# Hybrid attention, DeltaNet and SSD step on one core: norms split around their root, pinned weight casts, three banks for turned tiles, sign and copies of the softmax stage

## The chip, the cores and the metric

One core of one Trainium2 chip runs the whole program. The metric is the device time of one execution in microseconds (us); the median of several executions counts. Matrix products run on TensorE (PE in the profile, its weight loads PEld), elementwise work on VectorE (DVE), ScalarE (ACT) and GpSimd (POOL); SyncE (SP) issues most transfers.

## The reference, cut to what matters

Two request groups, 128 context tokens and 512 latent tokens, pass through the same two layers with the same weights (model width 1024, fp32):

```python
for layer in range(DEPTH):
    h = modulate(x, norm_mix_g[layer], sh1, sc1)      # rms_norm(x) * gain * (1 + scale) + shift
    y = even_mixer(h) if layer % 2 == 0 else odd_mixer(h)
    x = x + g1 * y
    h = modulate(x, norm_mlp_g[layer], sh2, sc2)
    x = x + g2 * (relu(h @ w_mlp_in) ** 2) @ w_mlp_out
return rms_norm(x, final_norm_g)
```

The even mixer joins grouped-query attention (8 heads of 64, 2 key heads; `softmax(q k * 64 ** -0.5) v`; latent queries see 512 latent and 256 cached keys) with a bidirectional gated DeltaNet (4 heads, state 128 x 128, a chunk recurrence in each direction). The odd mixer is a bidirectional Mamba-2 SSD. Besides the two outputs the new caches and states are returned.

## The kernel before, in words

Tokens are 5 tiles of 128 (tile 0 is context). Every large product is computed in three passes from a split of each fp32 operand into a rounded high part and a remainder: high by high, high by low, low by high. For weights, `wpart` (L267) makes the high part on ACT (L272) and the remainder on DVE (L275). `gemm` (L291, products L300) makes feature-major outputs of 128 rows for half of the tokens; `by_rows` (L317, products L328) makes token-major outputs, 512 columns at a time.

**Norms between blocks.** In the last pass of a `by_rows` with `done`, the 24 products of one token tile t run, then `gated` (L357) multiplies the PSUM result by the gate (L363, or L365) and adds it to x (L366), ACT squares x and sums the row (L381), and `done(t)` (L415) runs. For t = 1, 2 and 4 it computes the reciprocal root of tiles 0 and 1, of tile 2, and of tiles 3 and 4 together: `root` (L383) is 12 DVE instructions on a column or two, each needing the one before (L384, L234, L235, three rounds of L237 to L239). `scaled` (L397) then writes, for each tile and half row, x * root * scale (L402) and adds the shift (L403). The half rows live in four buffers. `turned` (L406) transposes a half row on PE in four pieces (L409) into one PSUM bank, copies it rounded on ACT (L412) and takes the remainder on DVE (L413). At t = 2 the half rows of tiles 0 and 1 are turned, at t = 3 those of tile 2; `late` (L428) turns tiles 3 and 4 between the first products of the next block.

This happens three times: after the even layer's output projection, where the bank of `turned` comes from a pool of two (L796, L797); after the first MLP, where `late` (the inner function, L828) prepares the odd layer's norm and the same lambda draws from a pool of one bank (L822); and after the odd layer's output projection, again with two (L1339, L1340). The next block's first products read the turned columns of tiles 0, 1 and 2.

**Order.** Each engine works through one queue in order. The queues are filled at build time by a scheduler that takes, among the instructions it holds to be ready, the one traced first; `issue_after(ins)` forces an instruction behind `ins` on its engine. Two engines that access the same PSUM bank are ordered by a semaphore.

**Attention and DeltaNet.** Both run in one stage: `attention` (L1211) is a generator whose steps are traced between the first DeltaNet head and the other three. For each of 4 pairs of heads it turns q (L1238 copies the result), and for each token tile computes scores into PSUM (L1243), the row maximum (L1249), its product with -scale (L1250), the exponential with row sums (L1252), the reciprocal (L1253) and the division (L1255); the probabilities are transposed (L1294) and copied out of PSUM alternately by DVE and ACT (L1297), then multiplied by v (L1303). The scores have one buffer and the transposes one bank. The probabilities' ring lies in the two landing buffers of the weights.

`delta_head` (L917) ends with the recurrence: per chunk and direction PE forms the new values in a bank (L1094, L1095), DVE makes a scaled copy `vk` (L1098) and a plain copy `vn` (L1100), PE multiplies `vk` by the keys into the other half of the same bank (L1102), and DVE updates the state (L1104); `vn` enters the output (L1107). The context chunk does the same (L1120, L1122, L1124, with the state copied by ACT at L1126).

Of the kernel before, what the change touches and what calls it, by code (L numbers as in the profile page):

```python
# [11 lines left out]
F32 = mybir.dt.float32  # L12
F32R = mybir.dt.float32r
I32 = mybir.dt.int32
AF = mybir.ActivationFunctionType
# [187 lines left out]
class Prog:  # L203
    def __init__(self, nc, tc, ctx, io, widx, pidx, cidx, csmall, taps=None):
        self.nc, self.tc, self.ctx, self.io = nc, tc, ctx, io
        self.turn, self.share = 0, False
        self.turns = [], None
        self.behind = None
        self.mlast = None
        self.widx, self.pidx, self.cidx, self.csmall = widx, pidx, cidx, csmall  # L210
        self.taps = taps or {}
# [55 lines left out]
    def wpart(self, raw, c, m=P, pool=None):  # L267

        pool = pool or self.wp
        hi = pool.tile([P, KT, m], F32R, name="whi", tag="whi")  # L270
        lo = pool.tile([P, KT, m], F32R, name="wlo", tag="wlo")
        self.nc.scalar.copy(out=hi, in_=raw[:, :, c:c + m])  # L272
        self.turn += 1
        eng = self.nc.gpsimd if self.share and self.turn % 2 else self.nc.vector
        eng.tensor_tensor(out=lo, in0=raw[:, :, c:c + m], in1=hi.bitcast(F32), op=ALU.subtract)  # L275
        return hi, lo
# [113 lines left out]
    def modulated(self, pool, scale, shift, h, off):  # L390


        nc, v = self.nc, self.nc.vector
        square, root = self.norm_rows(pool)
        todo = []

        def scaled(t, r):  # L397
            q = min(t, 1)
            for j in range(2):
                y = self.wp.tile([P, 512], F32, name="hrow", tag="hrow", bufs=4)  # L400
                c = slice(j * 512, j * 512 + 512)
                v.scalar_tensor_tensor(out=y, in0=self.x[:, t, c], scalar=r[:, t:t + 1], in1=scale[:, q, c], op0=ALU.mult, op1=ALU.mult)  # L402
                v.tensor_tensor(out=y, in0=y, in1=shift(q, j), op=ALU.add)  # L403
                todo.append((t, 4 * j, y))

        def turned(t, a, y):  # L406
            ps = self.bank("hps")
            for k in range(4):
                nc.tensor.transpose(ps[:, k * P:(k + 1) * P], y[:, k * P:(k + 1) * P], self.ident)  # L409
            ps = ps.rearrange("p (k c) -> p k c", c=P)  # L410
            hi, lo = (x[:, a:a + 4, off[t]:off[t] + P] for x in h)
            self.mlast = nc.scalar.copy(out=hi, in_=ps)  # L412
            v.tensor_tensor(out=lo, in0=ps, in1=hi.bitcast(F32), op=ALU.subtract)  # L413

        def done(t):  # L415
            if t in (2, 3):
                while todo:
                    turned(*todo.pop(0))
            if t in (1, 2, 4):
                a = 2 if t == 2 else t - 1  # L420
                r = root(a, t + 1)
                for u in range(a, t + 1):
                    scaled(u, r)
            self.turns = todo, turned

        return square, done
# [285 lines left out]
    def even(self):  # L712
# [108 lines left out]
        with ExitStack() as e1:  # L821
# [6 lines left out]
            def late():  # L828
                for _ in side:
                    pass  # L830
                shift, scale = (self.bands(mraw.tile([P, 2048], F32, name="bands", tag="wraw").rearrange("p (q c) -> p q c", q=2), 1, kind) for kind in (0, 1))
                self.padding(np_, h)
                square, done = self.modulated(np_, scale, lambda q, j: shift[:, q, j * 512:j * 512 + 512], h, TOFF)
                sq.append(square)
                return done
# [81 lines left out]
    def delta_head(self, dn, pd, h, st_, gt):  # L917
# [171 lines left out]
        for n in range(4):  # L1089
            for d in range(2):  # L1090
# [8 lines left out]
                vn = dn.tile([P, P], F32, name="vn", tag=f"vn{d}", bufs=2)  # L1099
                v.tensor_copy(vn, pv[:, 0:P])  # L1100
                if n < 3:
# [14 lines left out]
        for d in range(2):  # L1116
# [4 lines left out]
            vn = dn.tile([P, P], F32, name="vn0", tag=f"vn{d}", bufs=2)  # L1121
            v.tensor_copy(vn, pv[:, 0:P])  # L1122
            vns.append(vn)
# [87 lines left out]
    def attention(self, at, psc, pacc, qkv, keys, ota):  # L1211
# [10 lines left out]
        def stacks(kv, pr):  # L1222
# [4 lines left out]
            for ts_ in ((0, 1), (2, 3), (4,)):  # L1227
# [7 lines left out]
                for j, t in enumerate(ts_):  # L1235
                    for i in range(2):
                        nc.tensor.transpose(pt[:, (i * n + j) * P:(i * n + j + 1) * P], hf[:, j, i], self.ident)
                nc.scalar.copy(out=qs[:, :, ts_[0] * P:(ts_[0] + n) * P], in_=pt[:, :2 * n * P].rearrange("p (i c) -> p i c", i=2))  # L1238
            return qs
# [5 lines left out]
        def softmax(sc, p):  # L1245

            n = sc.shape[1]
            mx, sm = (at.tile([P, 2], F32, name=m, tag=m, bufs=3)[:, :n] for m in ("amx", "asm"))
            v.tensor_reduce(out=mx, in_=sc, axis=AX.X, op=ALU.max)  # L1249
            v.tensor_scalar(out=mx, in0=mx, scalar1=-scale, scalar2=None, op0=ALU.mult)  # L1250
            for i in range(n):
                nc.scalar.activation(out=p[:, i], in_=sc[:, i], func=AF.Exp, scale=scale, bias=mx[:, i:i + 1], accum_out=sm[:, i:i + 1])  # L1252
            v.reciprocal(out=sm, in_=sm)  # L1253
# [7 lines left out]
        for kv in range(2):  # L1261
            for pr in range(2):
# [17 lines left out]
                for t in range(1, NT):  # L1280
# [9 lines left out]
                    for j in range(3):  # L1290
# [5 lines left out]
                        turn += 1  # L1296
                        (v.tensor_copy if turn % 2 else nc.scalar.copy)(out=dst, in_=quad(pt))  # L1297
                    yield
# [446 lines left out]
```

## Time and profile before

| what | value |
|---|---|
| median of 3 runs | 2155.83 us (2148.13 to 2157.08) |
| the profiled execution's own time | 2143.07 us |
| its span, first to last instruction | 2141.2 us |
| mean granted TensorE clock | 0.968 |
| PE busy | 2029.4 us (95%) |
| DVE busy | 1376.8 us (64%) |
| ACT busy | 935.4 us (44%) |

A busy PE is a PE with a product in its pipe, not one at its peak. The granted clock is 1.00 at 2.4 GHz and 0.50 at 1.2 GHz; values between are a stretch with both.

### The profile page before, as it was taken

The page shows a single profiled execution, that of the slowest core. Times are in us where ns is not written, and L with a number is a line of the kernel's source. Part 1 is how long each engine was busy: PE and PEld are TensorE (multiplying, and loading weights), DVE is VectorE, ACT ScalarE, POOL GpSimd, SP SyncE. Part 2 cuts the span into 40 slices and gives each one's busy share as a digit, 9 for nine tenths or more (in the row PEclk, how much of TensorE's full clock was granted, in tenths as well). Part 3 has the DMA queues.
Part 4 walks back from the last instruction along what each step waited for, and adds up shares of the span by engine and source line. Part 5 has one row for each costly group of instructions (what it writes and reads, how often), then busy time and mean ns, then how long its engine had stood idle before and what let it go on. Part 6 is the DMA issues. An engine that isn't in the chain of part 4 may idle for free.

```text
span 2141.2 us, 32845 instructions
## 1 busy us (share of the span) xinstructions
PE 2029.4 (95%) x13227; PEld 1827.7 (85%) x13227; DVE 1376.8 (64%) x2628; ACT 935.4 (44%) x1959; POOL 147.3 (7%) x106
## 2 busy tenths in 40 slices
PE   6999698898899999999899999999999899999998
PEld 4989686775797989898799999999888888989896
DVE  6386777874886767664678886787634634343445
ACT  4344457573342423233259866666531332323131
POOL 1031302100000000000000001111110000000000
PEclk9999789898999999999999999999999999999999
DMA  7261101005255343332234343333341221212121
GB/s 328 85 241 40 38 1 35 1 12 198 100 188 190 134 148 136 141 124 95 89 101 148 129 146 120 114 133 126 117 159 67 91 97 60 79 60 99 59 79 50
DMA packets 55834, 233.31 MB, mean 109 GB/s; under 512 B 6074, under 2 KB 21186, under 8 KB 33922
## 3 DMA queue, kind: packets, MB, share of 16 engines
q1 hardware_dynamic: 45952, 216.63, 28.4%
q10 hardware_dynamic: 9730, 14.58, 1.9%
q8 instruction: 104, 1.70, 0.3%
q14 instruction: 48, 0.39, 0.1%
HBM read 222.76 MB, written 8.43 MB: 108 GB/s over the span
## 4 chain that ended last, share of the span: by engine, by line
PE 85%; DVE 9%; DMA 2%; ACT 2%; issue 1%; POOL 0%; ACTq 0%; SPq 0%; DVEq 0%; POOLq 0%
PE gps L300 41%; PE rps L328 28%; PE yps L1648 2%; PE atps L750 2%; PE offps L1662 1%; PE scps L1243 1%; PE dps L1032 1%; DMA X<-growd 1%; PE stps L1679 1%; DMA wraw<-wall 1%; PE avps L1303 1%; PE dps L1038 1%; PE ptps L1294 1%; DVE wlo L275 1%; PE xkps L1498 1%
## 5 line engine op out<-in xcount | busy, mean ns | idle before, releaser
L300 PE MATMUL gps<-hh,whi 128*128 128x322 f32 (+3 forms) x1552 | 488.6, 316 | 1.4 <-ACT hh L412 1.4
L300 PE MATMUL gps<-hh,wlo 128*128 128x322 f32 (+3 forms) x1552 | 486.5, 314 | 0.0
L300 PE MATMUL gps<-hl,whi 128*128 128x322 f32 (+3 forms) x1552 | 485.6, 313 | 0.0
L300 PEld LDWEIGHTS gps<-hh,whi 128*128 128x128 f32 (+1 forms) x1552 | 292.3, 189 | 7.9 <-issue 5.1
L300 PEld LDWEIGHTS gps<-hl,whi 128*128 128x128 f32 (+1 forms) x1552 | 292.4, 188 | 3.2 <-issue 2.8
L300 PEld LDWEIGHTS gps<-hh,wlo 128*128 128x128 f32 (+1 forms) x1552 | 292.4, 188 | 2.1 <-issue 1.7
L328 PE MATMUL rps<-wlo,hidh 128*128 128x512 f32 x640 | 253.3, 396 | 0.0
L328 PE MATMUL rps<-whi,hidh 128*128 128x512 f32 x640 | 252.3, 396 | 0.0
L328 PE MATMUL rps<-whi,hidl 128*128 128x512 f32 x640 | 250.5, 395 | 0.0
L272 ACT CAST whi<-wraw 128x1024 fp32r<-128x1024 f32 (+2 forms) x132 | 140.3, 1065 | 247.1 <-PE rps L328 176.3
L284 DVE TENSOR_TENSOR wlo<-wraw,whi 128x1024 fp32r<-128x1024 f32 x88 | 107.4, 1225 | 191.5 <-ACT whi L283 191.5
L300 PE MATMUL gps<-yh,whi 128*128 128x320 f32 x1024 | 227.1, 311 | 0.2 <-ACT yh L412 0.2
L275 DVE TENSOR_TENSOR wlo<-wraw,whi 128x1024 fp32r<-128x1024 f32 (+3 forms) x123 | 157.8, 1283 | 100.7 <-ACT whi L272 100.3
L283 ACT CAST whi<-wraw 128x1024 fp32r<-128x1024 f32 x88 | 91.8, 1049 | 269.6 <-PE rps L328 188.5
L300 PEld LDWEIGHTS gps<-yh,whi 128*128 128x128 f32 x1024 | 172.6, 189 | 1.0 <-ACT yh L412 0.7
L300 PE MATMUL gps<-yh,wlo 128*128 128x320 f32 x512 | 158.6, 310 | 0.0
L328 PEld LDWEIGHTS rps<-whi,hidh 128*128 128x128 f32 x640 | 120.3, 188 | 29.3 <-issue 1.2
L328 PEld LDWEIGHTS rps<-wlo,hidh 128*128 128x128 f32 x640 | 120.3, 188 | 28.8 <-issue 0.6
L328 PEld LDWEIGHTS rps<-whi,hidl 128*128 128x128 f32 x640 | 120.3, 188 | 28.6
L485 DVE SCALAR_TENSOR_TENSOR macc<-wraw,condst,macc 128x512 f32<-128x512 f32 x196 | 137.2, 752 | 5.6 <-ACT macc L488 5.6
L650 DVE TENSOR_SCALAR hr<-gps 128x320 f32<-128x320 f32 x128 | 62.9, 492 | 105.7 <-PE gps L300 105.6
L651 ACT ACTIVATE hr<-hr 128x320 f32<-128x320 f32 x128 | 60.2, 470 | 150.8 <-DVE hr L650 149.3
(412 smaller groups left out, 3509.7 us busy)
## 6 DMA issues: line engine op xcount, KB each, us to landing
wraw<-wall SPq DMA_DIRECT2D x158, 1024.0 KB
bc<-afs SPq DMA_DIRECT2D x40, 512.0 KB
Q<-afr SPq DMA_DIRECT2D x64, 128.0 KB
xt<-xt ACTq DMA_DIRECT2D x1, 2560.0 KB
X<-growd SPq DMA_DIRECT2D x8, 320.0 KB
x<-x ACTq DMA_DIRECT2D x1, 2560.0 KB
xd<-x ACTq DMA_DIRECT2D x1, 2560.0 KB
x<-xd SPq DMA_DIRECT2D x1, 2560.0 KB
```

The costliest lines, as they stand in the source:

```text
L272: self.nc.scalar.copy(out=hi, in_=raw[:, :, c:c + m])
L275: eng.tensor_tensor(out=lo, in0=raw[:, :, c:c + m], in1=hi.bitcast(F32), op=ALU.subtract)
L283: self.nc.scalar.copy(out=hi, in_=x)
L284: self.nc.vector.tensor_tensor(out=lo, in0=x, in1=hi.bitcast(F32), op=ALU.subtract)
L300: self.nc.tensor.matmul(ps, ws[k // KT][q // 2][:, k % KT, :], xs[q % 2][k][:, c], start=k == 0 and q == 0, stop=k == n - 1 and q == 2)
L328: nc.tensor.matmul(ps, parts[x][k][:, c], w[y][:, j, :], start=k == 0 and q == 0, stop=k == n - 1 and q == 2)
L485: nc.vector.scalar_tensor_tensor(out=a, in0=x, scalar=w, in1=a, op0=ALU.mult, op1=ALU.add)
L650: nc.vector.tensor_scalar(out=r, in0=ps, scalar1=0.0, scalar2=None, op0=ALU.max)
L651: nc.scalar.activation(out=r, in_=r, func=AF.Square)
L750: nc.tensor.matmul(ps[:, :n], x[k][:, TOFF[t]:TOFF[t] + P], w[:, k, :], start=k == 0 and q == 0, stop=k == KT - 1 and q == 2)
L1032: nc.tensor.matmul(py[:, t * 32:(t + 1) * 32], m32[:, t, :], mixed(Xc, t, l), start=True, stop=True)
L1648: nc.tensor.matmul(py[q * 64:q * 64 + 64, pr * P:(pr + 1) * P], X[t](1 + d)[:, hh * 64:hh * 64 + 64], D[t][:, d, hh, :], start=d == 0, sto ...
```

## The change

In `scaled`, x * scale is computed first, for all half rows of the call, before `root` is; then one instruction multiplies by the root and adds the shift. At t = 4 four of these last instructions are kept, and the next four calls of `wpart` have their DVE remainder forced behind them: two behind tile 2's second half row, two behind tile 3's. For the norm after the first MLP, `turned` takes banks in turn from three pools (one bank, one bank, and the products' pool of six). In the softmax stage q is multiplied by -scale when it is copied out of PSUM, so that the scores are negative: the row minimum is then the bias itself and the product at L1250 is gone. `vn` is copied by ACT, and three of four copies of the transposed probabilities are ACT's.

```diff
@@ wpart
-        eng.tensor_tensor(out=lo, in0=raw[:, :, c:c + m], in1=hi.bitcast(F32), op=ALU.subtract)
+        with self.tc.issue_after(self.hold.pop(0).ins) if self.hold else nullcontext():
+            eng.tensor_tensor(out=lo, in0=raw[:, :, c:c + m], in1=hi.bitcast(F32), op=ALU.subtract)
@@ modulated
-        todo = []
-        def scaled(t, r):
-            q = min(t, 1)
-            for j in range(2):
-                y = self.wp.tile([P, 512], F32, name="hrow", tag="hrow", bufs=4)
-                c = slice(j * 512, j * 512 + 512)
-                v.scalar_tensor_tensor(out=y, in0=self.x[:, t, c], scalar=r[:, t:t + 1], in1=scale[:, q, c], op0=ALU.mult, op1=ALU.mult)
-                v.tensor_tensor(out=y, in0=y, in1=shift(q, j), op=ALU.add)
+        todo, held = [], []
+        def scaled(a, b):
+            ys = []
+            for t in range(a, b):
+                for j in range(2):
+                    y = self.wp.tile([P, 512], F32, name="hrow", tag="hrow", bufs=4)
+                    c = slice(j * 512, j * 512 + 512)
+                    v.tensor_tensor(out=y, in0=self.x[:, t, c], in1=scale[:, min(t, 1), c], op=ALU.mult)
+                    ys.append((t, j, y))
+            r = root(a, b)
+            for t, j, y in ys:
+                last = v.scalar_tensor_tensor(out=y, in0=y, scalar=r[:, t:t + 1], in1=shift(min(t, 1), j), op0=ALU.mult, op1=ALU.add)
                 todo.append((t, 4 * j, y))
+                if t > 1:
+                    held.append(last)
@@ modulated, done
             if t in (1, 2, 4):
-                a = 2 if t == 2 else t - 1
-                r = root(a, t + 1)
-                for u in range(a, t + 1):
-                    scaled(u, r)
+                scaled(2 if t == 2 else t - 1, t + 1)
             self.turns = todo, turned
+            if t == NT - 1:
+                self.hold = [held[1], held[1], held[2], held[3]]
@@ even, late
+                banks = cycle(((self.pn, "n"), (self.pmod, "mod"), (self.pg, "g")))
+                def bank(name):
+                    pool, tag = next(banks)
+                    return pool.tile([P, 512], F32, name=name, tag=tag)
+                self.bank = bank
@@ delta_head
-                v.tensor_copy(vn, pv[:, 0:P])
+                nc.scalar.copy(out=vn, in_=pv[:, 0:P])
...
-            v.tensor_copy(vn, pv[:, 0:P])
+            nc.scalar.copy(out=vn, in_=pv[:, 0:P])
@@ attention
-                nc.scalar.copy(out=qs[...], in_=pt[...])
+                nc.scalar.activation(out=qs[...], func=AF.Copy, scale=-scale, in_=pt[...])
...
-            v.tensor_reduce(out=mx, in_=sc, axis=AX.X, op=ALU.max)
-            v.tensor_scalar(out=mx, in0=mx, scalar1=-scale, scalar2=None, op0=ALU.mult)
+            v.tensor_reduce(out=mx, in_=sc, axis=AX.X, op=ALU.min)
             for i in range(n):
-                nc.scalar.activation(out=p[:, i], in_=sc[:, i], func=AF.Exp, scale=scale, bias=mx[:, i:i + 1], accum_out=sm[:, i:i + 1])
+                nc.scalar.activation(out=p[:, i], in_=sc[:, i], func=AF.Exp, scale=-1.0, bias=mx[:, i:i + 1], accum_out=sm[:, i:i + 1])
...
-                        (v.tensor_copy if turn % 2 else nc.scalar.copy)(out=dst, in_=quad(pt))
+                        (nc.scalar.copy if turn % 4 else v.tensor_copy)(out=dst, in_=quad(pt))
```

## Rows read from the trace of the kernel before

**Rows 1.** The page, busy time of each engine over the span.
```profile
PE 2029.4 (95%) x13227; PEld 1827.7 (85%) x13227; DVE 1376.8 (64%) x2628; ACT 935.4 (44%) x1959; POOL 147.3 (7%) x106
```

**Rows 2.** Stages: length; PE, PEld, DVE, ACT, POOL busy (instructions); clock, DMA share, GB/s.
```profile
226.00:502.00 276.00, 230.97 (x1599) 197.09 (x1599) 207.65 (x587) 166.05 (x415) 47.47 (x36) 0.85 0.09 28
...
1685.00:2130.00 445.00, 444.76 (x2472) 401.25 (x2472) 193.01 (x317) 126.48 (x209) 0.00 (x0) 1.00 0.20 70
```

**Rows 3.** The same view at the three norms between blocks.
```profile
567.00:574.00 7.00, 0.16 (x1) 0.19 (x2) 6.96 (x18) 2.25 (x5) 0.00 (x0) 0.87 0.50 186
...
576.00:579.00 3.00, 3.00 (x13) 3.00 (x13) 2.97 (x7) 0.40 (x1) 0.00 (x0) 0.50 0.00 0
...
1042.00:1045.00 3.00, 0.11 (x2) 0.00 (x0) 3.00 (x6) 1.17 (x3) 0.00 (x0) 1.00 0.00 0
...
1053.00:1057.00 4.00, 3.70 (x15) 3.30 (x16) 3.31 (x6) 1.19 (x2) 0.00 (x0) 0.51 0.02 4
...
1668.00:1676.00 8.00, 1.12 (x10) 0.80 (x7) 7.93 (x21) 3.01 (x6) 0.00 (x0) 0.71 0.94 393
```

**Rows 4.** Timeline of DVE at the first norm: start, duration, instruction, [idle before].
```profile
560.96 0.15 DVE L384 SCALAR_TENSOR_TENSOR nms<-nss 128x1 f32<-128x1 f32 x1
...
562.10 1.23 DVE L275 TENSOR_TENSOR wlo<-wraw,whi 128x1024 fp32r<-128x1024 f32 x1 [0.62 <-ACT whi L272]
...
564.88 1.28 DVE L413 TENSOR_TENSOR hl<-hps,hh 128x512 fp32r<-128x512 f32 x2
...
571.60 1.42 DVE L402 SCALAR_TENSOR_TENSOR hrow<-x,nr,spare 128x512 f32<-128x512 f32 x2
...
573.00 1.29 DVE L403 TENSOR_TENSOR hrow<-hrow,shift 128x512 f32<-128x512 f32 x2
```

**Rows 5.** Timeline of PE at the first norm.
```profile
573.84 1.94 PE L409 MATMUL hps<-con,hrow 128*128 128x128 f32 x8 [6.93 <-DVE hrow L403]
...
575.60 1.44 PE L300 MATMUL gps<-hh,whi 128*128 128x320 f32 x4
```

**Rows 6.** Timeline at the third norm: DVE's root of tile 2, PE's next transposes.
```profile
1662.71 0.16 DVE L384 SCALAR_TENSOR_TENSOR nms<-nss 128x1 f32<-128x1 f32 x1
...
1676.24 1.94 PE L409 MATMUL hps<-con,hrow 128*128 128x128 f32 x8 [7.12 <-DVE hrow L403]
```

**Rows 7.** Timeline at the second norm: PE's transposes, ACT's weight cast, PE's products.
```profile
1045.08 0.63 PE L409 MATMUL hps<-con,hrow 128*128 128x128 f32 x4 [2.96 <-DVE hl L413]
...
1056.40 2.01 ACT L272 CAST whi<-wraw 128x1024 fp32r<-128x1024 f32 x2 [1.40 <-DVE hrow L403]
...
1059.58 0.39 PE L300 MATMUL gps<-hh,whi 128*128 128x322 f32 x1
```

**Rows 8.** Waits of the attention and DeltaNet stage: us in total, times, longest.
```profile
ACT p L1252 <- DVE amx L1250: 13.8, 12, 3.7
```

**Rows 9.** Timeline of DVE in that stage, one row maximum.
```profile
317.76 0.96 DVE L1249 TENSOR_REDUCE amx<-scps 128x1 f32<-128x768 f32 x1
...
319.80 0.15 DVE L1250 TENSOR_SCALAR amx<-amx 128x1 f32<-128x1 f32 x1
```

**Rows 10.** Groups by line, that stage: busy us, mean ns, idle before and its releaser.
```profile
L1255 ACT ACTIVATE p<-p,asm 128x768 f32<-128x768 f32 x32 | 30.1, 940 | 10.8 <-DVE asm L1253 10.7
...
L1297 DVE COPY pp<-ptps 128x512 f32<-128x512 f32 x16 | 11.0, 687 | 1.2 <-PE ptps L1294 0.9
...
L1297 ACT COPY pp<-ptps 128x512 f32<-128x512 f32 x16 | 9.3, 582 | 11.0 <-PE ptps L1294 11.0
L1100 DVE COPY vn<-dps 128x128 f32<-128x128 f32 x32 | 9.1, 284 | 0.8 <-PE dps L1095 0.8
...
L1250 DVE TENSOR_SCALAR amx<-amx 128x1 f32<-128x1 f32 (+1 forms) x36 | 6.2, 173 | 0.3
...
L1126 ACT COPY s<-dps 128x128 f32<-128x128 f32 x8 | 2.1, 261 | 2.2 <-PE dps L1124 2.2
```

**Rows 11.** Groups by line, whole run: two engines on one PSUM bank.
```profile
L874 DVE COPY dk<-kvps 128x128 f32<-128x128 f32 x20 | 5.7, 286 | 8.1 <-ACT djk L873 8.1
```

More of the change, by code (lines that the diff above doesn't have):

```diff
@@ L2 @@
 from types import SimpleNamespace
-from itertools import islice
+from itertools import cycle, islice
 import numpy as np
@@ L207, in __init__ @@
         self.turns = [], None
+        self.hold = []
         self.behind = None
@@ L1237, in stacks @@
                         nc.tensor.transpose(pt[:, (i * n + j) * P:(i * n + j + 1) * P], hf[:, j, i], self.ident)
-                nc.scalar.copy(out=qs[:, :, ts_[0] * P:(ts_[0] + n) * P], in_=pt[:, :2 * n * P].rearrange("p (i c) -> p i c", i=2))
+                nc.scalar.activation(out=qs[:, :, ts_[0] * P:(ts_[0] + n) * P], func=AF.Copy, scale=-scale, in_=pt[:, :2 * n * P].rearrange("p (i c) -> p i c", i=2))
             return qs
```

## Prediction

> **What bounds the kernel now.** I read the page first: PE has a product in its pipe for 95% of the span, DVE is at 64% and ACT at 44% [rows 1]. The stages say where the other 5% lies. From 1685 us on PE is busy for 444.76 of 445 us at full clock [rows 2]: nothing that DVE or ACT does there can give time back. The change touches the two kinds of place where PE is not full: the attention and DeltaNet stage (226 to 502 us, PE 231 of 276 us, granted clock 0.85, so 1.2 GHz for part of it) [rows 2], and the three norms between blocks. There PE does 0.16 us in 7 us, 0.11 in 3 us and 1.12 in 8 us, while DVE has 6.96, 3.00 and 7.93 us of work; after the gap the clock is granted at 0.50 or 0.51, which is 1.2 GHz [rows 3]. So in the norms DVE sets the time, and the question is which of its instructions PE is waiting for.
>
> **First and third norm.** PE's gap is 6.93 us and ends with the half rows of tile 2 [rows 5]. Their root starts at 560.96 and the second half row ends at 573.00 + 1.29 = 574.29, 13.3 us later [rows 4]. The chain itself is short: 12 instructions of 0.15 us that follow each other some 0.2 us apart, 2.3 us, and 1.42 + 1.29 = 2.7 us for two half rows. In between lie the four weight remainders of the next block at 1.23 us, 4.9 us, slipped in between dependent root instructions, four L413 remainders (two times 1.28 us) and one gate pair, about 1.4 us (an L402 pair's time) [rows 4]. The change forces two of the L275 behind the second half row and two behind tile 3's, and does tile 2's first pass over x (1.4 us) ahead of the root: 4.9 + 1.4 = 6.3 us sooner. Tiles 0 and 1 have their first passes (four, 2.7 us) moved ahead of their root as well, which can bring tile 2 forward by up to that: 9.0 us at most. The instruction count stays the same; the fused instruction merely changes place.
>
> What is late next: the products need the first remainder too. Both remainders behind tile 2 (2.5 us) now stand before or between its two L413 (1.3 us), so the first product comes up to 3 us after the half row where it came 575.60 - 574.29 = 1.3 us after [rows 4, 5]. That gives 6.3 - 1.7 = 4.6 us at the low end; at the high end PE's own gap of 6.93 us and a slow pair of transposes (1.94 us, half of it clock) stop it near 8. I take 5, near the low end, because DVE had no idle time there to hide anything in. The half clock lasts from 573.84 to about 579 [rows 3, 5], which costs some 2.5 us; PE was idle in 1042 to 1045 too and the clock was still 1.00 there [rows 3], so a shorter gap may lose less, and I count 1 us. The other two remainders wait for tile 3: gate pair 1.4, square and sum under 1, root 2.3, half row 0.7, remainder 1.2, some 6.5 us after PE's last product, and are needed after 48 products, 48 x 444.76 / 2472 = 8.6 us after the first [rows 2]. That is hidden; without that cover it costs 1 to 2 us. No transfer is moved, but a weight landing buffer is held until its remainder is made, so the third and fourth loads of the block start a few us later; their weights are needed only after eight groups of 24 products, 35 us, which hides it. The third norm repeats the pattern: 13.5 us from root to transposes, a gap of 7.12 us [rows 6]. So **6 us each, bounds 3 to 9**.
>
> **Second norm.** Here six half rows pass through one bank, and each group of transposes waits for the L413 before it, 2.96 us at 1045.08 [rows 7]. Then the next block's weight cast at 1056.40 waits for the last half row of tile 4, because its landing place is the bands' [rows 7], and the next products start at 1059.58, 18 us after PE's last full run ends near 1042. With three banks the transposes of tiles 0 and 1 no longer wait, but DVE's sum of work is the same, and it is 100% busy in 1042 to 1045 [rows 3]. What can go is its idle time and the first passes that move forward, as above 2.7 us or so, and PE can put the small product and the last transposes into that time. Bounds: 2 us (DVE alone decides) and 9 us (half of the 18). I take 5, and 1 us of the clock, which stood at 0.51 from 1053 to 1057 [rows 3]: **6 us, bounds 2 to 10**. The three norms together: 18 us, 8 to 28.
>
> **Attention and DeltaNet.** L1250 goes: 36 x 0.173 = 6.2 us off DVE [rows 10]. More counts where it sits: the row maximum ended at 317.76 + 0.96 = 318.72 but L1250 ran at 319.80, behind other work in DVE's queue [rows 9]; ACT stood idle for 13.8 us in all for this one instruction before the exponential [rows 8]. Scores have one buffer, so each exponential holds back the next scores. Between 0 (PE, 84% busy, covers it) and 13.8 us I take 7, the middle.
>
> `vn` moves: 40 x 0.284 = 11.4 us off DVE, 40 x 0.261 = 10.4 us onto ACT [rows 10]. Before, it ran on the same engine right behind `vk`. The second product of the bank must wait for both. Two engines that read one bank are ordered: L874 on DVE stood idle for 8.1 us behind ACT's L873, of which it needs nothing but the bank [rows 11]. So ACT's `vn` waits for DVE's `vk`, and behind it in ACT's queue stand exponentials and divisions of the other chain. It cannot be a gain on that link; it costs nothing if ACT is free, and 0.94 us if an L1255 is in front [rows 10]: 0 to 37.6 us over 40. I take 2 us, close to L1126, a copy of that shape on ACT [rows 10], because most of the links have PE work of another chain beside them.
>
> Of 48 copies of probabilities 12 move: 12 x 0.687 = 8.2 us off DVE, 12 x 0.582 = 7.0 us onto ACT [rows 10]. They are hidden beside PE's other chain; if that cover is gone, each costs up to 0.94 us, 11 us. The copy itself is 15% shorter on ACT [rows 10]. The Trainium skill, in "Trainium Architecture — The Big Picture", section "The five engines, in one table", says that ScalarE is not for simple arithmetic, VectorE being up to about three times faster per element. By that, as an estimate, 12 copies of 2.1 us and 40 of 0.85 us would put 59 us onto ACT instead of 17, and the stage would lose perhaps 15 us; the rows disagree for copies out of PSUM, and the rows decide.
>
> The stage's balance: DVE 207.65 - 25.8 = 182 us, ACT 166.05 + 17.4 = 183 us of 276 [rows 2]. Neither is a bound. The sign in q's copy and the minimum instead of the maximum cost nothing: same instructions, same sizes. Net **5 us faster, bounds 14 faster to 12 slower**.
>
> **Sum.** 18 + 5 = 23 us off the profiled execution's own 2143.07 us: 2120. That execution lies 12.8 us under the median of the runs shown, 2155.83 us; against the median it is 2133 us, and that is my forecast, 1.1% faster. About 0.5% (11 us) is what a measurement of this kernel can tell from no change.
>
> **Rivals.**
> (a) DVE keeps the norms. For it: DVE busy 6.96 of 7 us and 7.93 of 8 [rows 3], and the remainders only move from before tile 2's half rows to between them and the products. Then each norm gives its low bound, 8 us in all, and attention nothing: 2148 us, no change. Against: 4.9 us of remainders for weights that PE reads later stand in front of the instruction that it waits for [rows 4]. The same result comes if the scheduler packs other work into the root's gaps. Chance 0.19.
> (b) `vn` on ACT takes the stage. Place: the link `vk`, `vn`, second product, 40 times, with ACT's queue in between. Price: up to 0.94 us each, 37.6 us [rows 10]; with the norms' 18 us that is 20 us slower, 2175 us. It makes the kernel slower by over 0.5% from a mean delay of (18 + 11) / 40 = 0.7 us per copy on. Against: ACT is idle for 40% of that stage [rows 2]. Chance 0.08. The Trainium skill, in "PSUM — Partial Sum Buffer", section "PSUM bank collisions raise a hardware error", says that any two engines in one bank and quadrant must be kept apart by software, two readers included; the trace agrees, with L874's 8.1 us [rows 11].
> (c) Attention is freed entirely (14 us) and the norms give their upper bounds (28 us): 2155.8 - 42 = 2114 us. For it: PE at 1.2 GHz for part of the stage would speed up as its gaps close. Chance 0.07.
>
> **How the numbers follow.** The forecast has 0.66. Faster by over 0.5% is the forecast and (c), 0.73; within 0.5% is (a), 0.19; slower is (b), 0.08. The range runs from (c), with 4 us of the runs' own spread below it, to 2153: norms at 8 us and `vn` costing a few us more than taken.
>
> **What would show it.** Right: in the norms no L275 between tile 2's root instructions, PE's gap before its transposes under 3 us instead of 6.93 and 7.12, no half clock of 5 us behind them; at the second norm the products starting 5 us sooner after the last run; ACT's wait on the minimum (L1249) well below 13.8 us; DVE's and ACT's busy time in the attention stage both near 183 us. Wrong: PE's gap unchanged but named after L275 or L413; waits of L1102 or L1124 on ACT's `vn` of more than 10 us; or a stage as long as before, because the heads and attention end together and freeing one leaves the other.

## The result, and the profile after

The changed kernel's median is 2126.54 us (2125.01 to 2136.3, six runs) where the kernel before had 2154.57 (six runs): **ratio 0.989, interval 0.9865 to 0.9916**. By the ratio that is 24 us less, by the medians 28. The forecast was 2133 us. The profiled execution took 2125.95 us, 17 us less than that of before (2143.07). Two executions among those below, one of the norms' edits alone (2287 us at a mean granted clock of 0.828) and one of the kernel before (3326 us at 0.554), are left out of the ratios.

The page, busy time of each engine [rows 1]:

```profile
PE 2027.7 (95%) x13227; PEld 1829.8 (86%) x13227; DVE 1354.7 (64%) x2540; ACT 942.5 (44%) x2011; POOL 142.3 (7%) x106
```

Where the 17 us lie is read from PE's products of `by_rows`, grouped by line: the first and the last start of each kind is a milestone. Those of the changed kernel (`op`: output projection of the even layer; `hidh`: second half of both MLPs; `yh`: output projection of the odd layer):

```profile
L330 PE MATMUL rps<-whi,hidh x640: 390/393/774, 623.8 to 2113.4; 128*128 128x512 f32 x160
...
L330 PE MATMUL rps<-whi,op x160: 387/394/497, 492.6 to 549.6; 128*128 128x512 f32 x160
L330 PE MATMUL rps<-whi,yh x160: 389/389/628, 1537.1 to 1653.5; 128*128 128x512 f32 x160
```

The same lines of the kernel before:

```profile
L328 PE MATMUL rps<-whi,hidh x640: 390/393/503, 638.6 to 2130.5; 128*128 128x512 f32 x160
...
L328 PE MATMUL rps<-whi,op x160: 387/394/796, 507.9 to 565.6; 128*128 128x512 f32 x160
L328 PE MATMUL rps<-whi,yh x160: 389/389/796, 1550.3 to 1667.4; 128*128 128x512 f32 x160
```

So there are four intervals: to the first `op` (the attention and DeltaNet stage ends there), from the last `op` to the first `hidh` (first norm), from there to the first `yh` (second norm and the odd layer), from the last `yh` to the last `hidh` (third norm and the second MLP):

| us | attention stage ends | first norm | second norm | third norm |
|---|---|---|---|---|
| before | 507.9 | 73.0 | 911.7 | 463.1 |
| changed | 492.6 | 74.2 | 913.3 | 459.9 |

The attention stage gave 15.3 us, the norms together 0.4, and the two output projections, which lie between the intervals, 0.7 each. The forecast had it the other way round: 5 from attention and 18 from the norms.

**The attention stage**, by stretches [rows 2], and, from the waits of the same stretch, ACT's for the minimum [rows 8]:

```profile
226.00:493.00 267.00, 229.37 (x1607) 197.76 (x1606) 182.09 (x479) 174.35 (x457) 47.09 (x36) 0.87 0.08 23
```
```profile
ACT p L1267 <- DVE amx L1265: 5.3, 7, 1.7
```

PE is without a product for 267.00 - 229.37 = 37.6 us; the kernel before, taken to its own end of the stage, for 48.8:

```profile
226.00:508.00 282.00, 233.20 (x1610) 197.62 (x1608) 208.84 (x590) 168.51 (x419) 47.47 (x36) 0.85 0.11 34
```

**The norms**, PE's timeline at the first, second and third [rows 5, 7, 6]:

```profile
554.74 1.94 PE L418 MATMUL hps<-con,hrow 128*128 128x128 f32 x8 [3.90 <-DVE hl L422]
556.50 1.43 PE L302 MATMUL gps<-hh,whi 128*128 128x320 f32 x4
...
575.71 1.09 PE L418 MATMUL hps<-con,hrow 128*128 128x128 f32 x4 [3.29 <-DVE hl L422]
...
1027.77 1.94 PE L418 MATMUL hps<-con,hrow 128*128 128x128 f32 x8 [4.46 <-DVE hrow L410]
1029.36 0.77 PE L330 MATMUL rps<-whi,hidh 128*128 128x512 f32 x1
...
1036.25 0.39 PE L330 MATMUL rps<-whi,hidl 128*128 128x512 f32 x1
...
1042.22 2.54 PE L418 MATMUL hps<-con,hrow 128*128 128x128 f32 x12 [2.09 <-DVE hrow L410]
...
1045.19 0.64 PE L302 MATMUL gps<-hh,whi 128*128 128x322 f32 x1
...
1659.45 1.94 PE L418 MATMUL hps<-con,hrow 128*128 128x128 f32 x8 [4.22 <-DVE yh L422]
```

and DVE's at the first [rows 4]:

```profile
542.08 0.16 DVE L386 SCALAR_TENSOR_TENSOR nms<-nss 128x1 f32<-128x1 f32 x1 [0.85 <-ACT rps L383]
...
548.51 1.41 DVE L410 SCALAR_TENSOR_TENSOR hrow<-hrow,nr,shift 128x512 f32<-128x512 f32 x2
549.84 2.35 DVE L277 TENSOR_TENSOR wlo<-wraw,whi 128x1024 fp32r<-128x1024 f32 x2
552.11 0.69 DVE L365 TENSOR_TENSOR rps<-rps,spare 128x512 f32<-128x512 f32 x1
552.71 1.28 DVE L406 TENSOR_TENSOR hrow<-x,spare 128x512 f32<-128x512 f32 x2
553.91 1.29 DVE L422 TENSOR_TENSOR hl<-hps,hh 128x512 fp32r<-128x512 f32 x2
```

No weight remainder stands between the root instructions of tile 2 any more: from its start to the end of the half rows it takes 7.8 us (542.08 to 549.92) instead of 13.3. But PE doesn't wait for these half rows: it waits for a bank. Tile 1's remainders (L422 at 553.91), which free it, stand behind the two held weight remainders, a gate and two first passes. At the second norm the transposes of tile 2 stand in PE's queue ahead of tile 4's products (1029.36), so PE waits 4.46 us in the middle of the pass. In the kernel before, the last product of tile 4 is

```profile
1041.28 0.39 PE L328 MATMUL rps<-whi,hidl 128*128 128x512 f32 x1
```

The next block's first products follow it 18.3 us later before (1059.58, [rows 7]) and 8.9 us later now (1036.25 to 1045.19). But measured from the first `hidh`, that last product comes after 402.7 us before and after 412.5 us now: the 9.4 us that were won behind the pass were lost inside it. The granted clock behind these gaps is 0.50 again, in the view by stretches [rows 3]:

```profile
555.00:558.00 3.00, 3.00 (x13) 2.78 (x13) 2.89 (x7) 2.13 (x5) 0.00 (x0) 0.50 0.47 194
570.00:575.00 5.00, 2.42 (x18) 2.19 (x16) 5.00 (x11) 2.46 (x7) 0.00 (x0) 1.00 0.63 261
575.00:580.00 5.00, 3.62 (x13) 3.25 (x14) 5.00 (x9) 1.51 (x3) 0.00 (x0) 0.52 0.62 213
...
1026.00:1029.00 3.00, 1.23 (x6) 1.26 (x7) 2.82 (x9) 0.11 (x1) 0.00 (x0) 0.50 0.00 0
```

In 570 to 580 lies a gap that the kernel before did not have: PE waits 3.29 us ahead of transposes (575.71). Tiles 3 and 4 are turned through a single bank there, and DVE makes the next layer's modulation products (L494) between their remainders; which of the two makes the gap is tried in part 5.

### The profile page after: what moved, and what is told of

Read it like the earlier page. It is cut to its first block, busy times and chain, and to the rows that moved or that the text cites. A ratio compares the mean times of both kernels' runs of the same rounds, so it can differ in the third digit from the quotient of the medians.

```text
span 2124.1 us, 32809 instructions
## 1 busy us (share of the span) xinstructions
PE 2027.7 (95%) x13227; PEld 1829.8 (86%) x13227; DVE 1354.7 (64%) x2540; ACT 942.5 (44%) x2011; POOL 142.3 (7%) x106
## 4 chain that ended last, share of the span: by engine, by line
PE 88%; DVE 8%; DMA 2%; ACT 2%; issue 1%; SPq 0%; DVEq 0%; ACTq 0%
PE gps L302 41%; PE rps L330 28%; PE yps L1663 2%; PE atps L759 2%; PE offps L1677 1%; DMA wraw<-wall 1%; PE dps L1054 1%; PE stps L1694 1%; PE dps L1048 1%; PE scps L1259 1%; DMA X<-growd 1%; PE avps L1318 1%; PE ptps L1309 1%; PE xkps L1513 1%; PE hps L418 1%
## 5 line engine op out<-in xcount | busy, mean ns | idle before, releaser
L494 DVE SCALAR_TENSOR_TENSOR macc<-wraw,condst,macc 128x512 f32<-128x512 f32 x196 | 136.3, 751 | 1.3 <-ACT macc L497 1.3
```

The costliest lines, as they stand in the source:

```text
L494: nc.vector.scalar_tensor_tensor(out=a, in0=x, scalar=w, in1=a, op0=ALU.mult, op1=ALU.add)
```

## The experiments

Each kernel was timed beside the kernel before on the same chip; a ratio with its 95% interval is against those runs. Where a stage or an interval is given in us, it is read from one profiled execution.

**1. The two halves of the change, each alone.** The first takes the last two parts of the diff (`delta_head` and `attention`), the second the other four (`wpart`, `modulated`, `done`, `late`).

> The kernel before with the edits of the attention and DeltaNet stage alone (negative scores, the plain copies vn on ACT, three of four copies of the turned probabilities on ACT); the norms stay as they were. Theory A (the trace of the changed kernel: the stage's end moved 15.4 us forward, the ends of the three norms moved +0.6, +1.8 and -3.2 us against it): the ratio is 0.992 to 0.994, 13 to 17 us less than before, and the stage from 226 us to the first product of the output projection lasts about 266 us as in the changed kernel, where it was 282. Theory B (the forecast's split, 5 us from this stage and 18 from the norms): the ratio is 0.997 to 0.998, and the stage is shorter in the changed kernel only because the scheduler ordered it anew when the norms changed.

Measured: 2127.34 us, **0.9891 (0.9866 to 0.9916)**, the whole gain of the change; the stage ends at 490.8.

> The kernel before with the edits of the norms alone (scale ahead of the root, four remainders pinned behind the half rows, three pools of banks at the second norm); attention and DeltaNet stay as they were. Theory A: the ratio is 0.998 to 1.001, at most 4 us less; the gap ahead of the first norm's products is shorter, and a second gap follows it at tiles 3 and 4; the second norm's products come no sooner. Theory B (the forecast): the ratio is 0.990 to 0.993, 18 us less. A ratio of 0.996 or less would mean that the norms give more than the milestones of one pair of traces showed.

Measured: 2146.59 us, **0.9983 (0.9955 to 1.0011)**, no difference that shows (the mean is 3.7 us less, and the interval includes no change). Its intervals are 73.3, 911.4 and 460.1 us: nothing at the first and second norm, 3.0 us at the third. Theory A holds.

**2. One attention edit at a time.**

```diff
-            v.tensor_reduce(out=mx, in_=sc, axis=AX.X, op=ALU.max)
-            v.tensor_scalar(out=mx, in0=mx, scalar1=-scale, scalar2=None, op0=ALU.mult)
+            v.tensor_reduce(out=mx, in_=sc, axis=AX.X, op=ALU.min)
```
(and the sign in q's copy and in the exponential, as in the change)

> The kernel before with the negative scores alone: the product with -scale on two columns is gone from DVE's queue between each row minimum and ACT's exponential, and q is scaled in its copy. Theory A1 (the stage waits for DVE as a whole, and each DVE instruction taken away pays in part): 32 x 173 ns = 5.5 us less busy DVE, and a stage some 4 to 9 us shorter, ratio 0.996 to 0.998. Theory A2 (the wait of ACT on this product, 13.8 us, was the stage's bound): the whole 12 to 16 us, ratio 0.993, and the two moves of copies add nothing to it. Theory A3 (ACT's queue only changes what it waits for): under 2 us.

Measured: 2130.14 us, **0.9902 (0.987 to 0.9934)**. The stage ends at 487.1; ACT's wait for the minimum is 8.0 us:

```profile
226.00:487.00 261.00, 223.12 (x1606) 189.95 (x1605) 197.73 (x536) 166.43 (x411) 47.60 (x36) 0.91 0.13 40
```

This edit alone carries the gain, as theory A2 said, though not for A2's reason alone: ACT's wait shrinks by 5.8 us, the stage by 21.

```diff
-                v.tensor_copy(vn, pv[:, 0:P])
+                nc.scalar.copy(out=vn, in_=pv[:, 0:P])
```

> The kernel before with the plain copies vn moved from DVE to ACT, and nothing else. Theory A1 (the stage waits for DVE as a whole): 9.1 us less busy DVE, a stage some 3 to 7 us shorter, ratio 0.997 to 0.999. The forecast took 2 us more (ratio 1.001), with 37.6 us as the outer end of the loss. A rival of A1: the move pays only where DVE is no longer needed between score and exponential, so alone it is neutral or up to 5 us slower, and the changed kernel's gain comes of the edits together.

Measured: 2138.51 us, **0.9955 (0.9928 to 0.9981)**: faster, so the forecast's loss of 2 us and rival (b) are out. Part 4 shows where its 9 us lie. With the other edits it adds nothing that can be measured: all three attention edits give 0.9891, the scores alone 0.9902.

**3. The product kept, but taken out of the chain.**

```diff
+            jk = at.tile([P, 2], F32, name="jk", tag="jk", bufs=3)[:, :n]
+            v.tensor_scalar(out=jk, in0=mx, scalar1=-scale, scalar2=None, op0=ALU.mult)
```

> The negative scores alone, and behind each row minimum a product of the same size as the one removed, written to a tile that nobody reads. DVE issues as many instructions as in the kernel before, but ACT's exponential no longer waits for this one. If the gain of the negative scores alone (ratio 0.990, the stage's end 20.8 us earlier) is the shorter chain from score to exponential, it stays: ratio 0.989 to 0.993, the stage 15 us shorter or more. If it is DVE's 5.5 us of busy time, it goes: ratio 0.998 to 1.000. If it is neither but the new order that the scheduler makes, the stage lands anywhere, and the ratio lies between 0.992 and 1.004 with no reason in the waits.

Measured: 2129.02 us, **0.9905 (0.9883 to 0.9926)**. DVE has its 36 products back and the gain stays, so it was the chain and not DVE's time. The chain can be measured: the 32 exponentials of the latent tiles start, summed, 40.4 us after the end of their maximum in the kernel before, 13.7 us after their minimum with the negative scores alone and 16.0 us with the spare product. PE's idle time in the stage stays small too (267.00 - 231.75 = 35.2 us):

```profile
226.00:493.00 267.00, 231.75 (x1605) 199.16 (x1603) 197.22 (x566) 162.85 (x407) 47.94 (x36) 0.85 0.08 23
```

How late the product can be shows where it is now free to be late. DVE's and ACT's timelines of this kernel:

```profile
249.06 0.95 DVE L1249 TENSOR_REDUCE amx<-scps 128x1 f32<-128x768 f32 x1
...
251.66 4.18 DVE L881 TENSOR_SCALAR dk<-dk,drs 128x128 f32<-128x128 f32 x5
...
255.99 0.14 DVE L1251 TENSOR_SCALAR jk<-amx 128x1 f32<-128x1 f32 x1
...
250.04 0.90 ACT L1253 ACTIVATE p<-scps,amx 128x768 f32<-128x768 f32 x1 [0.43 <-DVE amx L1249]
```

The product comes 6 us after its minimum, behind DeltaNet's work in DVE's queue; the exponential has long run. In the kernel before, the 36 products end 33.4 us in all after their maxima (0.93 us each on average, 4.03 at most; [rows 9] is one of them), although they are busy for 6.2 us.

**4. The same work in another order, and the kernel before once more.**

```diff
-                        (v.tensor_copy if turn % 2 else nc.scalar.copy)(out=dst, in_=quad(pt))
+                        (nc.scalar.copy if turn % 2 else v.tensor_copy)(out=dst, in_=quad(pt))
```

> The kernel before with the alternate copies of the turned probabilities swapped: DVE makes those that ACT made and ACT those that DVE made, as many each. No work is added, removed or moved on balance, so each theory of work or of waits expects a ratio of 0.999 to 1.001 and a stage that ends within 3 us of the kernel before's 507.9 us. If the order that the scheduler makes of the same work is worth several us by itself, the stage's end moves by 4 us or more, and gains of that size from single edits of this stage are not to be read as prices of the edits.

Measured: 2151.42 us, **1.0002 (0.9981 to 1.0022)**. The median doesn't move, but the stage of the profiled execution ended at 518.7, 10.8 us later: this execution, the longest of its twelve (2156.12 us), and the median disagree.

> The kernel before, unchanged, for a second profile. Its executions lie between 2140 and 2164 us, while most of the changed kernel's lie within 2.3 us. If the spread is the clock granted in the attention stage, this execution's stage from 226 us to the first product of the output projection differs from 282 us by about as much as its whole time differs from 2143 us, and the intervals behind the stage (57.7 us of output projection, 73 us to the first MLP's second half, 463 us at the end) agree within 1 us. If the spread lies elsewhere, the stage lasts 282 us again and another interval differs.

Measured: 2158.48 us, 15.4 more than in the first profile. The stage ends at 523.1, 15.2 later; the other intervals are 72.9, 911.9 and 463.1 us, equal within 0.2. The 15 us between these two executions lie in this one stage, as expected:

```profile
226.00:523.00 297.00, 247.10 (x1599) 210.71 (x1597) 209.38 (x589) 167.93 (x418) 46.19 (x36) 0.81 0.10 32
```

PE is without work for 49.9 us, as in the first profile (48.8); its busy time is 14 us longer at a lower clock (0.81, not 0.85). Read that way, all profiled stages fall into two groups:

| kernels | PE idle in the stage, us | PE busy, us |
|---|---|---|
| before, before again, norms alone, `vn` alone, swapped copies | 48.8, 49.9, 49.6, 45.9, 42.5 | 233, 247, 230, 227, 250 |
| with negative scores: alone, with the spare product, all attention edits, changed kernel | 37.9, 35.2, 37.4, 37.6 | 223, 232, 228, 229 |

Those of the kernels of part 5 lie at 34.7 to 37.8 us idle. The negative scores take some 10 us of idle time out of PE (means 47.3 and 37.0); the rest of the difference between two executions is the clock granted while it works.

All executions bear this out, as an estimate. The 54 of the kernel before that enter the ratios of these parts take 2150.2 us on average at a mean granted clock of 0.966, and a line through them gives 1.86 us for each 0.001 of clock. With the negative scores alone the mean is 21.1 us less: 10.6 us below that line, that is at equal clock, and 10.5 us by a higher clock (0.972). `vn` alone is 9.0 us faster, but only 0.8 at equal clock; the rest is its clock (0.970). The swapped copies are 6.9 us faster at equal clock, and a lower clock (0.962) takes it back. So a new order of the same work can by itself be worth some 7 us of idle time, and one kernel's 10 us would not be proof. What speaks for the edit is that all nine profiles with negative scores have 34.7 to 37.9 us idle and all five without have 42.5 to 49.9, and that the exponentials lag by 12.7 to 18.4 us in the nine and by 40.0 to 43.9 in the five. Why a shorter chain, or `vn` on ACT, is granted a higher clock was not settled.

**5. The negative scores with the norms' edits, and the norms mended.** First the changed kernel with two parts undone:

```diff
-                nc.scalar.copy(out=vn, in_=pv[:, 0:P])
+                v.tensor_copy(vn, pv[:, 0:P])
...
-                        (nc.scalar.copy if turn % 4 else v.tensor_copy)(out=dst, in_=quad(pt))
+                        (v.tensor_copy if turn % 2 else nc.scalar.copy)(out=dst, in_=quad(pt))
```

> The changed kernel without the two moves of copies to ACT: negative scores and the norms' edits. If the two moves cost what the stage of the two earlier runs says (490.8 us with them, 487.1 us without), it is 2 to 5 us faster than the changed kernel: ratio 0.986 to 0.990. If the moves of copies carry part of the gain, it is slower than the changed kernel's 0.989, at 0.991 to 0.994.

Measured: 2125.32 us, **0.9893 (0.9871 to 0.9915)**: the same as the changed kernel. The two moves of copies neither cost nor bring anything that shows.

The next kernel takes away what the trace named:

```diff
-            if t in (2, 3):
+            if t in (2, NT - 1):
                 while todo:
                     turned(*todo.pop(0))
...
-                self.hold = [held[1], held[1], held[2], held[3]]
+                self.hold = [last[0], last[0], held[2], held[3]]
...
-                    v.tensor_tensor(out=y, in0=self.x[:, t, c], in1=scale[:, min(t, 1), c], op=ALU.mult)
+                    with self.tc.issue_after(low[0].ins) if t > 2 else nullcontext():
+                        v.tensor_tensor(out=y, in0=self.x[:, t, c], in1=scale[:, min(t, 1), c], op=ALU.mult)
...
-        self.bank = lambda name: self.pn.tile([P, 512], F32, name=name, tag="n")
+        self.bank = self.cycled((("pn", "n"), ("pg", "g")))
...
-                if side:
+                if side:
+                    owed += 1
+                while owed and not self.turns[0]:
+                    owed -= 1
                     next(side, None)
```
(`last[0]` and `low[0]` are tile 2's last remainder, L422; `cycled` takes banks in turn from the named pools)

> As the kernel with the negative scores and the norms' edits, with the three causes that the trace shows at the norms taken away: tile 2's half rows are turned behind tile 4's products, in banks of two or three pools at all three norms; the first two remainders of the weights and the products with scale of tiles 3 and 4 are put behind tile 2's last remainder; the modulation steps of the first two weight blocks of the first MLP come a block later, so that their products on DVE start behind the turned tiles. If those were what kept the norms' gain away, the gap ahead of the products shrinks to some 3 us at each norm, no second gap follows the first, and it is 6 to 14 us faster than the kernel with negative scores and the norms' edits as they are: ratio 0.980 to 0.985. If the queue of DVE simply has that much to do between the last product and the next (8 us at each norm, the forecast's first rival), it is within 3 us of that kernel.

Measured: 2113.79 us, **0.9836 (0.9815 to 0.9857)**, faster than the changed kernel too. Intervals 67.7, 907.2 and 459.4 us: 5.3, 4.5 and 3.7 us less than before, 13.5 in all, where the forecast gave 18 to the norms. PE's timeline at the three norms:

```profile
551.56 0.42 PE L302 MATMUL gps<-hh,whi 128*128 128x320 f32 x1 [1.84 <-DVE hl L427]
555.10 0.63 PE L302 MATMUL gps<-hh,wlo 128*128 128x320 f32 x1 [2.39 <-DVE wlo L277]
...
1026.89 0.53 PE L302 MATMUL gps<-hh,wlo 128*64 128x322 f32 x1 [2.88 <-DVE wlo L277]
...
1648.49 0.63 PE L302 MATMUL gps<-yh,wlo 128*128 128x320 f32 x1 [3.28 <-DVE wlo L277]
```

No transposes wait at the first norm any more; the second half of the wait is now for the weights' remainder. In front of it DVE makes the first passes of tiles 3 and 4:

```profile
551.42 2.49 DVE L411 TENSOR_TENSOR hrow<-x,spare 128x512 f32<-128x512 f32 x4
553.83 2.35 DVE L277 TENSOR_TENSOR wlo<-wraw,whi 128x1024 fp32r<-128x1024 f32 x2
```

So those went behind their root again:

```diff
+            if a < 3:
+                scales()
             r = root(a, b)
+            if a == 3:
+                scales()
```
(`scales` is the loop of first passes)

> The kernel with the three causes taken away, and one more: in its trace the four products with scale of tiles 3 and 4 (2.49 us on DVE) stand between tile 2's last remainder and the weights' remainders, and PE waits for those (2.39, 2.88 and 3.28 us at the third product of the three norms). Here the products of tiles 3 and 4 stand behind their root again, as in the kernel before. If that wait is on the path, 2 us at each norm: 4 to 8 us faster than the kernel with the three causes taken away, ratio 0.980 to 0.982. If the wait only moves (to the turned tiles 3 and 4, which then come 2.5 us later), within 2 us of its 0.9836.

Measured: 2115.58 us, **0.9856 (0.9829 to 0.9882)**, the same within the intervals. The waits for the weights' remainder shrank, from 2.39, 2.88 and 3.28 us to none, none and 0.97. The first interval gained 3.0 us (64.7), the others nothing (907.5, 459.9); at the third norm PE waits 2.71 us for a half row instead, and where the second norm's went was not followed. The stage of this execution ended 6.7 us later. So the first expectation holds at one norm of three. The same with the first diff of this part reversed:

> The same with the two moves of copies to ACT as in the changed kernel. The three attention edits together ended the stage at 490.8 us, the negative scores alone at 487.1. If the moves cost those 3.7 us, the ratio is 0.002 above the one without them. If stage ends 4 us apart are within what the granted clock does to this stage, the two agree within 0.001 to 0.002 in either direction.

Measured: 2118.24 us, **0.987 (0.9848 to 0.9892)**: within 0.002 of the one without the moves. Its stage ended at 489.6, its second interval is 911.1; what that one lost was not followed.

Last, the mended kernel of 2113.79 us with one part of its diff taken back:

```diff
-                if side:
-                    owed += 1
-                while owed and not self.turns[0]:
-                    owed -= 1
+                if side:
                     next(side, None)
```

> The kernel with the three causes taken away, but with the modulation steps of the first MLP where the changed kernel has them. From the end of the output projection's products to the first product of the MLP's second half the changed kernel takes 74.2 us and the one with the three causes taken away 67.7. If the products of the modulation on DVE in front of tile 3's and 4's remainders are what makes the second gap, this kernel takes 70 to 73 us there, with PE waiting for turned tiles near 570 us, and is 2 to 5 us slower than the one with them later: ratio 0.985 to 0.986. If the banks and the pinned order were enough, it takes 67 to 69 us, and the ratio is 0.983 to 0.984.

Measured: 2115.45 us, **0.9829 (0.9798 to 0.9861)**; the first interval is 67.9 us, as with the steps later. The modulation products stand between the remainders as in the changed kernel and the second gap is gone all the same. That theory falls: with more banks and the new order of transposes, DVE's modulation products there cost PE nothing that shows. What the single bank, the order of the transposes and the pinning cost apart from each other was not tried. The best versions are this one and the one it was made from, both 1.6 to 1.7% under the kernel before.

## Why the prediction was right, and where it was wrong

**The total** was right (2133 us forecast, 2126.5 measured, range 2110 to 2153), and that was luck: two errors cancelled. The forecast's 23 us were split 18 to 5, the measured ones some 3 to 21.

**The attention term was mis-sized: 5 us, measured some 21 to 23** (ratios 0.9902 and 0.9891). The step that failed is "Between 0 and 13.8 us I take 7, the middle". It priced the removed product by ACT's idle time named after it [rows 8]. PE's idle time fell by some 10 us, so this part of the step was inside its bounds and 3 us too small. As much again came from the clock granted to PE while it works, and the term put that at nothing; only rival (c) said that PE at 1.2 GHz would speed up as its gaps close, and its bound of 14 us was too low for both together. The wait named in a profile counts only what was left when ACT had nothing else to do: the products' own delay was 33.4 us, which [rows 9] showed once and the prediction quoted (318.72 to 319.80) without summing, and the exponentials came 26.7 us sooner. The bound "12 slower" of the same term follows from none of its parts; `vn` alone has 37.6 us there.

**`vn` on ACT** (2 us lost, up to 37.6): the sign was wrong. PE's wait for it ahead of the second product is 0.5 us in all in the changed kernel, where it was 1.4 us for DVE's copy in the kernel before:

```profile
L1118 PEld LDWEIGHTS dps<-vk,dk 128*128 128x128 f32 x48 | 7.2, 190 | 0.8 <-ACT vn L1116 0.5
```

The ordering of two engines in one bank, which cost 8.1 us in [rows 11], costs next to nothing here. DVE's busy time of 182 us in the stage came as forecast. ACT's 174 is 9 us under the forecast's 183: the moved copies took 10.7 and 7.6 us there, as worked out (10.4 and 7.0); what else went from ACT's busy time was not followed.

**The norms' term was mis-sized: 18 us, measured 3 to 4** (ratio 0.9983, whose interval includes no change; by the milestones +0.3, -0.3 and -3.0). The root became shorter as worked out, 13.3 to 7.8 us (5.5, forecast 6.3). What failed is "what is late next": it counted the two held remainders ahead of tile 2's L413 and missed two things in the same queue, the gate with two first passes of tiles 3 and 4, and tile 1's remainders, which free the bank of tile 2's transposes. The gap fell from 6.93 to 3.90 us, not under 3. "That is hidden" for tiles 3 and 4 failed: a second gap of 3.29 us follows it. The half clock came back behind both (0.50 from 555 to 558, 0.52 from 575 to 580). At the second norm the sign named in advance came true, the products start 9 us sooner after the last run, and yet nothing was won: the transposes that PE was to put into the waiting time stand ahead of tile 4's products, so the last run itself ends 9.8 us later. Rival (a) described this outcome, and its 8 us lie inside the measured interval, whose lower end is 10 us.

With the transposes later, more banks and another pinning the same edits gave 13.5 us (part 5). The Trainium skill, "Perfetto Trace Analysis", section "Identifying Performance Opportunities" (its "Optimization Strategy"), says that a repeated gap on the engine that should be full can mean that there is no PSUM free for the next tile. The trace agrees: 3.90, 3.29 and 4.22 us ahead of transposes, all named after the remainder that frees a bank, and no such wait is left in the kernel that has more banks, though its transposes and pinned remainders were moved as well.

**The base.** The prediction saw that the profiled execution lay 12.8 us under the median and carried that over as a constant. The second profile, 15.4 us longer, shows where such a difference lies: in the attention stage. The changed kernel's profile lies at its median (2125.95 and 2126.54), which is why the medians differ by 28 us and the profiles by 17.

## What to carry to other kernels

An instruction in a chain delays its consumer by the time from its input's end to its own end in its engine's queue, not by its duration. Sum that over all its occurrences (here 33.4 us, where the durations are 6.2 and the wait named after it 13.8). Here that sum bounded the gain and was not its price: the consumers came 26.7 us sooner, PE's idle time fell by 10, and the time by 21, half of it through the granted clock. When something is moved behind the instruction that PE waits for, list everything that then stands between that instruction and PE's next one, remainders that free a PSUM bank included. A gap that shrinks is won only if the work ahead of it has not grown: measure from a point before both. Before a profile is used as a base, ask in which stage it differs from the median.

## What was not expected of the hardware

PE can have a product in its pipe for a whole stretch and be granted half the clock. In the kernel with swapped copies:

```profile
416.00:426.00 10.00, 10.00 (x45) 9.61 (x45) 5.13 (x10) 3.56 (x6) 0.00 (x0) 0.50 0.00 0
426.00:436.00 10.00, 10.00 (x48) 9.81 (x46) 5.83 (x14) 4.16 (x9) 0.00 (x0) 0.50 0.00 0
```

In the first profile of the kernel before the stretch from 416 to 436 us, with PE busy for 17.24 of 20 us, is at 1.00 throughout. By the two profiles of the kernel before, the clock of this stage alone makes two executions of one kernel differ by 15 us. What decides it was not settled. The Trainium skill, "Perfetto Trace Analysis", section "Identifying the Most-Contended Engine", warns that TensorE's busy share does not say how close it is to its peak; these two rows agree: 93 products start in these 20 us, where the kernel before has 164 (not the same ones).
